# The down projection of a feed-forward block as seven products, each summed over all 22 row blocks in PSUM

## The chip, the cores and the metric

The kernel runs on one core of a Trainium2 chip. The core's engines run in parallel, each with a queue of its own in program order: TensorE (PE) multiplies matrices, VectorE (DVE) and ScalarE (ACT) work on tiles in SBUF and PSUM, GpSimd (POOL) on tiles in SBUF, and SyncE (SP) issues most of the DMA transfers. The metric is the device time of one execution in microseconds (us). All arithmetic is float32, and what a matrix multiplication reads is split into two parts of lower precision.

## The reference

A trunk of two layers on 1024 positions with 1024 features: a token mixer, a cross-attention into a memory of 256 rows, and a feed-forward block, each inside RMS norms. The change touches the feed-forward block, which each layer runs once, with `D_FF` = 2816:

```python
def rms_norm(x, g):
    return x * lax.rsqrt(jnp.mean(x * x, axis=-1, keepdims=True) + RMS_EPS) * g

def swiglu_ffn(x, w_in, w_out):
    gate, up = jnp.split(x @ w_in, 2, axis=-1)
    return (jax.nn.silu(gate) * up) @ w_out

for i in range(2):
    ...
    h = swiglu_ffn(rms_norm(x, g[4]), ffn_w_in[i], ffn_w_out[i])
    x = x + rms_norm(h, g[5])
```

Here g stands for the gains of layer i.

## The kernel before

**Up projection** (`ffn`, L440). The 2816 hidden features are 22 blocks m of 128. For each, `block(m)` makes gate and up for all 1024 positions by 84 matmuls of 128x512 (`mm7`, L438): a 2x2 block product done by seven products instead of eight, with sums and differences of the weights made on POOL (L466 to L469). The gated block, 128 features by 1024 positions, goes to DRAM in two DMAs of 256 KB each (L530), one for each half a of the positions within a tile pair.

**Down projection** (`ffn_out`, L550). It multiplies the gated H (1024 positions by 2816 features) by `w_out` (2816 by 1024). It is again a 2x2 block product by seven products: positions are split into tiles 2j and 2j+1 (a = 0, 1), features into two halves b of each group, output columns into two halves c of 512. The loop over groups is the outer one (L556): six groups of 2, 4, 4, 4, 4 and 4 row blocks. A group loads four H tiles (L564) and four W tiles (L567), and POOL makes four left combinations (L573, L575, L577, L579) and four right ones (L574, L576, L580, and L587 when product 4 is built). `unit(i)` splits the two operands of product i into a high part (a cast on ACT, L118) and a low part (a subtraction on DVE, L119). `mm` (L606) then multiplies, per j and per row block pair, three times: high by high, high by low, low by high. Within a group products follow in the order 1, 5, 6, 3, 7, 2, 4; some share a PSUM bank, and after each one of them the bank is added into the SBUF tiles `y` by DVE (L615; by an ACT copy, L612, where the output has nothing yet). The last group has j as its outer loop, and `finish` follows each output half: a sum of squares on ACT (L619) and a multiplication by the post-norm gain on POOL (L620; for the very last tile on DVE). `close` (L363) then loads the residual rows, adds (L378) and stores them. In the first layer it goes on to the next pre-norm and transposes; tiles are closed in pairs there, and one by one in the second layer.

**What sets the order.** Each engine's queue is written by a scheduler at build time from the program's order and the pools: `wr` has 3 buffers of 512 KB, `wp` 4 of each kind (wh and wl), `t4` 4, `s7` 2, A 32, PSUM 8 banks of 128x512. `later` queues small pieces of other work (the closes; `mem_in`, which normalizes and transposes the memory rows for the next layer), and `tick` lets them go on by a piece between products. `mk` starts `mem_in(1)` when the closer of the first layer's block is made, which is at the start of the last group.

Of the kernel before, what the change touches and what calls it, by code (L numbers as in the profile page):

```python
# [21 lines left out]
class Trunk:  # L22
# [332 lines left out]
    def closer(self, gpost_row, xin, xout, gpre):  # L355
# [3 lines left out]
        ready = [[], []]  # L359
# [3 lines left out]
        def close(tiles, hs, s):  # L363
# [30 lines left out]
            ready[half] += hs  # L394
# [3 lines left out]
            yield from (self.turn7 if s7_in else self.turn)(half, ready[half], gpre)  # L398
# [41 lines left out]
    def ffn(self, w_in, w_out, mk_close):  # L440
# [3 lines left out]
        hd = [self.dram([P, 2, 4, P]) for _ in range(NF)]  # L444
# [26 lines left out]
        w = lambda W, n: W[n] if isinstance(W[n], tuple) else unit(W[n])  # L471

        def block(m):
# [45 lines left out]
            nc.gpsimd.tensor_mul(h1, h1, u3)  # L519
# [8 lines left out]
            nc.vector.tensor_mul(h0, h0, a)  # L528
            for i in range(2):
                nc.sync.dma_start(hd[m][:, i], ht.rearrange('f (q a t) -> f a q t', q=4, a=2)[:, i])  # L530
# [17 lines left out]
        self.ffn_out(hd, w_out, mk_close)  # L548

    def ffn_out(self, hd, w_out, mk_close):  # L550

        nc = self.nc
        sizes = [1] + [2] * 5
        y, m0 = (None, 0)
        view = lambda t, K: t[:, :K * 512].rearrange('p (k c) -> p k c', k=K)
        for gi, K in enumerate(sizes):  # L556
            first, last = (gi == 0, gi == len(sizes) - 1)
            n = K * 512
            H, W = ({}, {})
            for b in range(2):  # L560
                for a in range(2):
                    H[a, b] = self.a32()
                    for k in range(K):
                        nc.sync.dma_start(H[a, b][:, k * 512:k * 512 + 512], hd[m0 + b * K + k][:, a].rearrange('f q t -> f (q t)'))  # L564
                    W[b, a] = self.wr.tile([P, D], F32, name='wr', tag='wr') if b else self.tmp()
                    r0 = (m0 + b * K) * P
                    nc.sync.dma_start(view(W[b, a], K), w_out[r0:r0 + K * P, a * 512:a * 512 + 512].rearrange('(k p) c -> p k c', p=P))  # L567
            H = {k: x[:, :n] for k, x in H.items()}
            W = {k: x[:, :n] for k, x in W.items()}
            E = nc.gpsimd  # L570
            s1, s2, s4 = [self.a32()[:, :n] for _ in range(3)]
            t1, t2 = [self.s7.tile([P, D], F32, name='s7', tag='s7')[:, :n] for _ in range(2)]
            E.tensor_add(s1, H[1, 0], H[1, 1])  # L573
            E.tensor_sub(t1, W[0, 1], W[0, 0])  # L574
            E.tensor_sub(s2, s1, H[0, 0])  # L575
            E.tensor_sub(t2, W[1, 1], t1)  # L576
            E.tensor_sub(s4, H[0, 1], s2)  # L577
            s3, t3, t4 = (H[1, 0], W[0, 1], W[1, 0])
            E.tensor_sub(s3, H[0, 0], s3)  # L579
            E.tensor_sub(t3, W[1, 1], t3)  # L580
            ops = {1: (H[0, 0], W[0, 0]), 5: (s1, t1), 6: (s2, t2), 3: (s4, W[1, 1]), 7: (s3, t3), 2: (H[0, 1], W[1, 0]), 4: (H[1, 1], t4)}
            units = {}

            def unit(i):
                if i not in units:
                    if i == 4:
                        E.tensor_sub(t4, t4, t2)  # L587
                    h, w = ops[i]
                    us = []
                    for j, x in enumerate((h, w)):  # L590
                        if j and (not (last and i in (7, 2, 4))):
                            hi = self.wp.tile([P, D], F32R, name='wh', tag='wh')
                            lo = self.wp.tile([P, D], F32R, name='wl', tag='wl')
                        else:
                            hi, lo = (self.a32r(), self.a32r())
                        self.split(hi[:, :n], lo[:, :n], x)
                        us.append((view(hi, K), view(lo, K)))
                    units[i] = us
                return units[i]

            def mm(ps, i, j, start):
                (hh, hl), (wh, wl) = unit(i)
                js = slice(j * P, (j + 1) * P)
                for k in range(K):
                    for q, (a, b) in enumerate(((hh[:, k, js], wh[:, k]), (hh[:, k, js], wl[:, k]), (hl[:, k, js], wh[:, k]))):
                        nc.tensor.matmul(ps, lhsT=a, rhs=b, start=start and k == 0 and (q == 0), stop=k == K - 1 and q == 2, skip_group_check=True)  # L606
            done = set()

            def add(t, c, ps):
                o = y[t][:, c * 512:c * 512 + 512]  # L610
                if first and (t, c) not in done:
                    nc.scalar.copy(o, ps)  # L612
                    done.add((t, c))
                else:
                    nc.vector.tensor_add(o, ps, o)  # L615

            def finish(t, c):
                o = y[t][:, c * 512:c * 512 + 512]
                nc.scalar.activation(self.junk, o, AF.Square, scale=1.0 / 32, accum_out=s3_[:, c:c + 1, t % nn])  # L619
                (nc.gpsimd if nn > 1 or (nn == 1 and t < 7) else nc.vector).tensor_mul(o, o, close.gpost[:, c * 512:c * 512 + 512])  # L620
# [1082 lines left out]
```

## Time and profile before

| | us |
|---|---|
| median of 3 timed executions | 3323.72 |
| lowest, highest | 3318.04, 3324.5 |
| the profiled execution | 3319.07 |
| its span, first to last instruction | 3317.1 |
| down projection, first layer | 1078.3 to 1343.0 |
| down projection, second layer | 3054.1 to 3307.7 |

The mean granted TensorE clock was 0.957. The profile gives, for each engine, the time that it was busy; a line such as L615 is a line of the kernel before. Groups of instructions name the operation with its output and inputs by tile names, the tile shape, the count, the busy time, the mean of one, and the idle time just before them with what ended it. In a list of waits "X <- Y" says that X stood idle until Y was done. "SPq" rows are DMA issues; the end of a transfer is seen in the instruction that waited for it.

### The profile page before, as it was taken

Reading aid. Unit: us, or ns where it says so; the run is one execution under the profiler, and the core shown is the slowest. Engines: PE = TensorE matmul, PEld = TensorE weight load, DVE = VectorE, ACT = ScalarE, POOL = GpSimd, SP = SyncE. Lnnn points to the kernel's source line nnn. Section 1 sums busy time; section 2 is a strip of 40 time slices with the busy share of each in tenths; the row PEclk is TensorE's granted clock in tenths of the full one; section 3 lists DMA queues with packets and bytes.
Section 4 is the critical chain, followed back from the end, with each engine's and each line's share of the span. In section 5 each row is a group of like instructions: output and inputs, shape, how many; then the busy total and the mean of one; then the engine's idle time right before and its main releaser. Section 6 shows DMA issues by size and latency. Waiting matters only on the chain. (4 is left out here: it accounts for less than half of the span.)

```text
span 3317.1 us, 44473 instructions
## 1 busy us (share of the span) xinstructions
PE 3155.1 (95%) x16586; PEld 2534.3 (76%) x16586; DVE 2023.3 (61%) x2875; ACT 1490.9 (45%) x2759; POOL 1062.2 (32%) x800
## 2 busy tenths in 40 slices
PE   8999999899999888999989999999999899999897
PEld 6888888678888666877668688787788688887666
DVE  5463545655444998755766375664545744445998
ACT  5443544533333433766753254465545533334332
POOL 0000011443334654311512242343011633334654
PEclk9999999999999999999998587899999999999999
DMA  5622544332223432744856443635544232323322
GB/s 185 203 76 70 197 146 141 113 96 83 76 77 89 140 102 76 246 126 130 286 176 171 139 106 83 168 93 175 172 159 157 65 96 83 87 79 115 108 96 95
DMA packets 446231, 421.44 MB, mean 127 GB/s; under 512 B 74560, under 2 KB 349152, under 8 KB 446016
## 3 DMA queue, kind: packets, MB, share of 16 engines
q1 hardware_dynamic: 439104, 393.44, 38.7%
q0 software_dynamic: 6912, 25.17, 2.3%
q8 instruction: 131, 2.15, 0.3%
q14 instruction: 84, 0.69, 0.1%
HBM read 313.61 MB, written 104.92 MB: 126 GB/s over the span
## 5 line engine op out<-in xcount | busy, mean ns | idle before, releaser
L438 PE MATMUL ps<-a,wh 128*128 128x512 f32 x2464 | 771.9, 398 | 6.9 <-DVE a L119 5.4
L119 DVE TENSOR_TENSOR wl<-wr,wh 128x1024 fp32r<-128x1024 f32 (+1 forms) x369 | 447.8, 1224 | 352.9 <-ACT wh L118 352.4
L118 ACT CAST wh<-wr 128x1024 fp32r<-128x1024 f32 (+1 forms) x369 | 323.4, 889 | 533.4 <-PE ps L438 179.9
L438 PEld LDWEIGHTS ps<-a,wh 128*128 128x128 f32 x2464 | 465.2, 189 | 123.8 <-DVE a L119 7.4
L438 PE MATMUL ps<-a,wl 128*128 128x512 f32 x1232 | 479.6, 397 | 0.0
L606 PE MATMUL ps<-wh,a 128*128 128x512 f32 x1136 | 381.8, 407 | 47.1 <-DVE a L615 31.6
L148 PE MATMUL ps<-a,wh 128*128 128x512 f32 (+1 forms) x848 | 333.9, 399 | 12.2 <-ACT a L118 8.6
L149 PE MATMUL ps<-a,wh 128*128 128x512 f32 (+2 forms) x848 | 328.7, 389 | 1.1 <-DVE a L119 1.1
L150 PE MATMUL ps<-a,wl 128*128 128x512 f32 (+2 forms) x848 | 327.6, 388 | 1.1 <-DVE wl L119 1.0
L148 PE MATMUL ps<-wh,a 128*128 128x512 f32 x800 | 313.8, 401 | 11.7 <-DVE a L415 7.7
L149 PE MATMUL ps<-wl,a 128*128 128x512 f32 x800 | 318.5, 398 | 0.0
L150 PE MATMUL ps<-wh,a 128*128 128x512 f32 x800 | 316.3, 399 | 0.0
L606 PEld LDWEIGHTS ps<-wh,a 128*128 128x128 f32 x1136 | 217.6, 192 | 123.3 <-DVE a L615 37.8
L438 PEld LDWEIGHTS ps<-a,wl 128*128 128x128 f32 x1232 | 233.1, 189 | 57.5 <-DVE wl L119 0.9
L119 DVE TENSOR_TENSOR wl<-s,wh 128x512 fp32r<-128x512 f32 (+1 forms) x200 | 207.6, 1050 | 76.7 <-ACT wh L118 73.8
L118 ACT CAST wh<-s 128x512 fp32r<-128x512 f32 (+1 forms) x200 | 129.7, 662 | 247.1 <-PE ps L438 86.8
L119 DVE TENSOR_TENSOR a<-a 128x1024 fp32r<-128x1024 f32 (+1 forms) x134 | 216.5, 1630 | 24.3 <-ACT a L118 20.8
L606 PE MATMUL ps<-wl,a 128*128 128x512 f32 x568 | 227.5, 401 | 0.0
L208 POOL TENSOR_TENSOR sm<-sm,mhalf 128x4 f32<-128x4 f32 (+3 forms) x60 | 67.8, 1133 | 489.1 <-DVE sm L228 423.6
L615 DVE TENSOR_TENSOR a<-ps,a 128x512 f32<-128x512 f32 x304 | 195.5, 680 | 13.8 <-PE ps L606 13.7
L148 PEld LDWEIGHTS ps<-a,wh 128*128 128x128 f32 x848 | 162.6, 193 | 50.7 <-ACT a L118 9.3
L118 ACT CAST a<-a 128x1024 fp32r<-128x1024 f32 (+1 forms) x150 | 125.3, 867 | 153.0 <-POOL a L577 53.5
(275 smaller groups left out, 5663.0 us busy)
## 6 DMA issues: line engine op xcount, KB each, us to landing
wr<-in_ffn_w_in SPq DMA_DIRECT2D x90, 512.0 KB
scr<-t SPq DMA_DIRECT2D x136, 256.0 KB
scr<-t SPq DMA_DIRECT2D x60, 512.0 KB
a<-scr SPq DMA_DIRECT2D x108, 256.0 KB
wr<-in_rw_w_rkv SPq DMA_DIRECT2D x48, 512.0 KB
t<-scr SPq DMA_DIRECT2D x36, 512.0 KB
ld<-scr SPq DMA_DIRECT2D x72, 256.0 KB
wr<-in_xa_wkv SPq DMA_DIRECT2D x32, 512.0 KB
```

The source lines that it names most:

```text
L118: self.nc.scalar.copy(hi, src)
L119: (engine or self.nc.vector).tensor_sub(lo, src, hi)
L148: nc.tensor.matmul(out, lhsT=ah, rhs=bh, start=start, stop=False)
L149: nc.tensor.matmul(out, lhsT=ah, rhs=bl, start=False, stop=False)
L150: nc.tensor.matmul(out, lhsT=al, rhs=bh, start=False, stop=stop)
L208: self.nc.gpsimd.tensor_tensor(out=r, in0=v, in1=self.mhalf[:, 0:n], op=ALU.pow)
L438: self.nc.tensor.matmul(out, lhsT=a, rhs=b, start=start and k == 0 and (i == 0), stop=k == 3 and i == 2, skip_group_check=True)
L606: nc.tensor.matmul(ps, lhsT=a, rhs=b, start=start and k == 0 and (q == 0), stop=k == K - 1 and q == 2, skip_group_check=True)
L615: nc.vector.tensor_add(o, ps, o)
```

## The change

`ffn_out` no longer loops over groups outside and products inside, but over products outside and steps inside. Each product (in the order 1, 2, 5, 6, 3, 7, 4) runs over six steps, one of one pair of row blocks and five of two, and stays in PSUM all the while; `evac` moves it out at its end. A bank that products share is read and then added to further. The W tiles stay in the A pool, and the right combinations are made in them by POOL as each product reaches them. The left combinations are made in the up projection by `out(m)`, once for each pair of row blocks, on POOL; H goes to seven DRAM tensors of 256 KB per pair, and a step loads the one that it needs through `wr`, three steps ahead. In the second layer product 4 runs tile by tile (j outermost), with its operands in the A pool. `finish` reads PSUM directly for product 4; `src is o` compares two slices made by separate calls. Closes come by even and by odd tiles in the first layer, so `ready` holds them by tile. `mem_in(1)` starts at product 7.

The diff, without `ffn_out`:

```diff
-        ready = [[], []]
+        ready = [{}, {}]
...
-            ready[half] += hs
+            ready[half].update(zip(tiles, hs))
             if len(ready[half]) < 4:
                 return
             self.fp32_in = fp32_in
-            yield from (self.turn7 if s7_in else self.turn)(half, ready[half], gpre)
+            yield from (self.turn7 if s7_in else self.turn)(half, [ready[half][t] for t in sorted(ready[half])], gpre)
             ready[half] = None
...
-    def ffn(self, w_in, w_out, mk_close):
+    def ffn(self, w_in, w_out, mk_close, late=None):
...
-        hd = [self.dram([P, 2, 4, P]) for _ in range(NF)]
+        hd = {i: self.dram([NF // 2, P, 512]) for i in range(1, 8)}
+        kept = {}
...
+        by_a = lambda x: x.rearrange('f (q a t) -> f a q t', a=2, t=P)
+
+        def gated(m, half):
+
+            if m not in kept:
+                kept[m] = self.a32()
+            return kept[m].rearrange('f (a q t) -> f a q t', a=2, t=P)[:, :, 2 * half:2 * half + 2]
+
+        def out(m):
+
+            c, x = m // 2, kept[m]
+            if m % 2 == 0:
+                nc.sync.dma_start(hd[1][c], x[:, :512])
+                return
+            e = kept.pop(m - 1)
+            del kept[m]
+            h00, h10, h01, h11 = (e[:, :512], e[:, 512:], x[:, :512], x[:, 512:])
+            nc.sync.dma_start(hd[2][c], h01)
+            nc.sync.dma_start(hd[4][c], h11)
+            cb = self.a32()
+            s1, s4 = (cb[:, :512], cb[:, 512:])
+            nc.gpsimd.tensor_add(s1, h10, h11)
+            nc.sync.dma_start(hd[5][c], s1)
+            nc.gpsimd.tensor_sub(h10, h00, h10)
+            nc.sync.dma_start(hd[7][c], h10)
+            nc.gpsimd.tensor_sub(h00, s1, h00)
+            nc.sync.dma_start(hd[6][c], h00)
+            nc.gpsimd.tensor_sub(s4, h01, h00)
+            nc.sync.dma_start(hd[3][c], s4)
...
-            nc.gpsimd.tensor_mul(h1, h1, u3)
+            nc.gpsimd.tensor_mul(gated(m, 1), by_a(h1), by_a(u3))
...
-            nc.vector.tensor_mul(h0, h0, a)
-            for i in range(2):
-                nc.sync.dma_start(hd[m][:, i], ht.rearrange('f (q a t) -> f a q t', q=4, a=2)[:, i])
+            nc.vector.tensor_mul(gated(m, 0), by_a(h0), by_a(a))
+            out(m)
...
-            if n == 2:
-                mem_in(1)
...
-        T.ffn(I['ffn_w_in'][i], I['ffn_w_out'][i], mk(3 * i + 2))
+        T.ffn(I['ffn_w_in'][i], I['ffn_w_out'][i], mk(3 * i + 2), None if i else lambda: mem_in(1))
```

And `ffn_out` as it is now, with the line numbers of the changed kernel:

```python
L579 def ffn_out(self, hd, w_out, mk_close, late):
L581     nc = self.nc
L582     steps = [(0, 1)] + [(c, 2) for c in range(1, D_FF // P // 2, 2)]
L583     NS = len(steps)
L584     seq = [(i, n) for i in (1, 2, 5, 6, 3, 7, 4) for n in range(NS)]
L585     view = lambda t, K: t[:, :K * 512].rearrange('p (k c) -> p k c', k=K)
L586     wv = w_out.rearrange('(c b p) n -> b p c n', b=2, p=P)
L587     W, H, U = ({}, {}, {})
L588     y = [self.a32() for _ in range(NT)]
L589     close = mk_close()
L590     nn = 2 if close.follow else 1
L592     def load(q):
L593         i, n = seq[q]
L594         c, K = steps[n]
L595         H[q] = self.wr.tile([P, D], F32, name='wr', tag='wr')
L596         nc.sync.dma_start(view(H[q], K), hd[i][c:c + K].rearrange('k f n -> f k n'))
L597         if i in (1, 2, 5, 6):
L598             b, a = {1: (0, 0), 2: (1, 0), 5: (0, 1), 6: (1, 1)}[i]
L599             W[b, a, n] = self.a32()
L600             nc.sync.dma_start(view(W[b, a, n], K), wv[b][:, c:c + K, a * 512:a * 512 + 512])
L602     def unit(q, resident=False):
L603         i, n = seq[q]
L604         K = steps[n][1]
L605         N = K * 512
L606         w = lambda b, a: W[b, a, n][:, :N]
L607         E = nc.gpsimd
L608         if i == 5:
L609             E.tensor_sub(w(0, 0), w(0, 1), w(0, 0))
L610         elif i == 6:
L611             E.tensor_sub(w(0, 0), w(1, 1), w(0, 0))
L612         elif i == 7:
L613             E.tensor_sub(w(0, 1), w(1, 1), w(0, 1))
L614         elif i == 4:
L615             E.tensor_sub(w(1, 0), w(1, 0), w(0, 0))
L616         src = {1: (0, 0), 5: (0, 0), 6: (0, 0), 2: (1, 0), 4: (1, 0), 3: (1, 1), 7: (0, 1)}[i]
L617         us = []
L618         for x in (H.pop(q)[:, :N], w(*src)):
L619             if resident:
L620                 hi, lo = (self.a32r(), self.a32r())
L621             else:
L622                 hi = self.wp.tile([P, D], F32R, name='wh', tag='wh')
L623                 lo = self.wp.tile([P, D], F32R, name='wl', tag='wl')
L624             self.split(hi[:, :N], lo[:, :N], x)
L625             us += [view(hi, K), view(lo, K)]
L626         U[q] = us
L628     def mm(ps, q, j):
L629         i, n = seq[q]
L630         hh, hl, wh, wl = U[q]
L631         js = slice(j * P, (j + 1) * P)
L632         for k in range(steps[n][1]):
L633             for z, (a, b) in enumerate(((hh[:, k, js], wh[:, k]), (hh[:, k, js], wl[:, k]), (hl[:, k, js], wh[:, k]))):
L634                 nc.tensor.matmul(ps, lhsT=a, rhs=b, start=i in (1, 2, 5) and n == 0 and k == 0 and z == 0, stop=n == NS - 1 and k == steps[n][1] - 1 and z == 2, skip_group_check=True)
L635     sums, done = ({}, {})
L637     def finish(t, c, src):
L639         group = (t % 2, t // 2 // nn)
L640         tiles = [2 * (group[1] * nn + g) + group[0] for g in range(nn)]
L641         if group not in sums:
L642             sums[group] = self.sums(nn)
L643             done[group] = 0
L644         s, s3 = sums[group]
L645         o = y[t][:, c * 512:c * 512 + 512]
L646         nc.scalar.activation(self.junk, src, AF.Square, scale=1.0 / 32, accum_out=s3[:, c:c + 1, tiles.index(t)])
L647         (nc.gpsimd if src is o else nc.vector).tensor_mul(o, src, close.gpost[:, c * 512:c * 512 + 512])
L648         done[group] += 1
L649         if done[group] == 2 * nn:
L650             self.later(close(tiles, [y[x] for x in tiles], s))
L652     def evac(i, j, A, B):
L653         o = lambda r, c: y[2 * j + r][:, c * 512:c * 512 + 512]
L654         if i == 1:
L655             nc.scalar.copy(o(0, 0), A)
L656         elif i == 2:
L657             nc.vector.tensor_add(o(0, 0), B, o(0, 0))
L658             finish(2 * j, 0, o(0, 0))
L659         elif i == 5:
L660             nc.scalar.copy(o(1, 1), B)
L661         elif i == 6:
L662             nc.scalar.copy(o(0, 1), A)
L663         elif i == 3:
L664             nc.vector.tensor_add(o(0, 1), B, o(0, 1))
L665             finish(2 * j, 1, o(0, 1))
L666         elif i == 7:
L667             nc.vector.tensor_add(o(1, 1), A, o(1, 1))
L668             finish(2 * j + 1, 1, o(1, 1))
L669         else:
L670             finish(2 * j + 1, 0, A)
L671     AHEAD = 3
L672     for q in range(AHEAD):
L673         load(q)
L674     unit(0)
L675     A, B = ([None] * 4, [None] * 4)
L676     by_tile = not close.follow
L677     for q, (i, n) in enumerate(seq):
L678         if q + AHEAD < len(seq):
L679             load(q + AHEAD)
L680         if q + 1 < len(seq):
L681             unit(q + 1, by_tile and seq[q + 1][0] == 4 and seq[q + 1][1] < NS - 2)
L682         if late and i == 7 and n == 0:
L683             late()
L684         if by_tile and i == 4:
L685             continue
L686         X = A if i in (1, 6, 7, 4) else B
L687         for j in range(4):
L688             if i in (1, 2, 5) and n == 0:
L689                 X[j] = self.bank()
L690             mm(X[j], q, j)
L691             if n == NS - 1:
L692                 evac(i, j, A[j], B[j])
L693             self.tick()
L694         del U[q]
L695     if by_tile:
L696         for j in range(4):
L697             for q in range(6 * NS, 7 * NS):
L698                 mm(A[j], q, j)
L699                 if q % 2:
L700                     self.tick()
L701             evac(4, j, A[j], None)
L702             self.tick(4)
```

Three lists show where the instructions go. The first is SyncE's queue around the end of the first layer's up projection, before: wr and t4 tiles are W loads, scr tiles H blocks in DRAM, the last one (scr32) of block 21.

```order
L567 DMA wr_8081<-in_ffn_w_out 128x512 [waits DMAHW5_49,DVE_49,Pool_49]
L567 DMA wr_8297<-in_ffn_w_out 128x2x512 [waits DMAHW0_49,DVE_49]
L567 DMA t4_8069<-in_ffn_w_out 128x512 [waits DMAHW7_49,DMAHW6_49,Pool_49]
L530 DMA scr31_5000<-t4_7830 128x4x128 [waits DVE_49]
L530 DMA scr31_5000<-t4_7830 128x4x128
L567 DMA t4_8073<-in_ffn_w_out 128x512 [waits DMAHW7_49,DMAHW1_49,DMAHW0_49]
L567 DMA t4_8287<-in_ffn_w_out 128x2x512 [waits DMAHW2_49,DMAHW6_49,DVE_49,Pool_49]
L567 DMA t4_8292<-in_ffn_w_out 128x2x512 [waits DMAHW3_49,Pool_49]
L567 DMA wr_8302<-in_ffn_w_out 128x2x512 [waits DMAHW4_49,DVE_49]
L530 DMA scr32_5001<-t4_7961 128x4x128 [waits DMAHW5_49,DVE_49]
```

The same place now: scr12 to scr17 are H operands of the products, a_8174 the W of the first step, a_8178 that of the second.

```order
L490 DMA scr12_4981<-a_8115 128x512 [waits DMAHW5_49,DVE_49]
L491 DMA scr14_4983<-a_8115 128x512 [waits DMAHW6_49]
L600 DMA a_8174<-in_ffn_w_out 128x512 [waits DMAHW7_49,PE_49]
L495 DMA scr15_4984<-a_8153 128x512 [waits DMAHW0_49,Pool_49]
L600 DMA a_8178<-in_ffn_w_out 128x2x512 [waits DMAHW1_49,DMASW2_49,PE_49]
L600 DMA a_8182<-in_ffn_w_out 128x2x512 [waits DMAHW2_49,PE_49]
L497 DMA scr17_4986<-a_7984 128x512 [waits DMAHW3_49,Pool_49]
L600 DMA a_8194<-in_ffn_w_out 128x2x512 [waits DMAHW4_49,PE_49]
```

W loads that stood ahead of the last block's store now stand behind the stores of the last pair, which wait for DVE and then for POOL.

The second is VectorE's queue in the first layer's down projection, before, in mid-projection: L119 are the splits, L615 the additions of PSUM banks (ps) into y (the a tiles).

```order
L615 TENSOR_TENSOR a_8101<-ps_8388,a_8101 128x512 [waits DVE_49,PE_49]
L119 TENSOR_TENSOR wl_8550<-wr_8297,wh_8549 128x1024 [waits Activation_49]
L615 TENSOR_TENSOR a_8096<-ps_8316,a_8096 128x512 [waits PE_49]
L119 TENSOR_TENSOR wl_8619<-t4_8584,wh_8618 128x1024 [waits Activation_49]
L615 TENSOR_TENSOR a_8098<-ps_8332,a_8098 128x512 [waits PE_49]
L119 TENSOR_TENSOR a_8615<-a_8581,a_8614 128x1024 [waits DMAHW5_49,DMAHW4_49,Activation_49]
L615 TENSOR_TENSOR a_8100<-ps_8340,a_8100 128x512 [waits PE_49]
```

The same queue now, at the end of product 2 and the start of product 5: L657 are additions of product 2 and L647 the multiplications by the gain (gb).

```order
L119 TENSOR_TENSOR wl_8582<-wr_8504,wh_8581 128x512 [waits DMAHW1_49,DVE_49,Activation_49]
L119 TENSOR_TENSOR wl_8586<-a_8174,wh_8585 128x512 [waits Activation_49]
L657 TENSOR_TENSOR a_8162<-ps_8416,a_8162 128x512 [waits PE_49]
L657 TENSOR_TENSOR a_8164<-ps_8420,a_8164 128x512 [waits PE_49]
L647 TENSOR_TENSOR a_8162<-a_8162,gb_8170 128x512 [waits Activation_49]
L657 TENSOR_TENSOR a_8166<-ps_8424,a_8166 128x512 [waits PE_49]
L647 TENSOR_TENSOR a_8164<-a_8164,gb_8170 128x512 [waits Activation_49]
L657 TENSOR_TENSOR a_8168<-ps_8428,a_8168 128x512 [waits PE_49]
L119 TENSOR_TENSOR wl_8633<-wr_8540,wh_8632 128x1024 [waits DMAHW2_49,Activation_49]
L647 TENSOR_TENSOR a_8166<-a_8166,gb_8170 128x512 [waits Activation_49]
L119 TENSOR_TENSOR wl_8637<-a_8178,wh_8636 128x1024 [waits Activation_49]
L647 TENSOR_TENSOR a_8168<-a_8168,gb_8170 128x512 [waits Activation_49]
```

The additions that alternated with splits throughout are gone from mid-product and stand in fours at a product's end, with the multiplications, which were POOL's.

More of the change, by code (lines that the diff above doesn't have):

```diff
@@ new lines, in ffn_out, with load @@
+        wv = w_out.rearrange('(c b p) n -> b p c n', b=2, p=P)
+        W, H, U = ({}, {}, {})
+        y = [self.a32() for _ in range(NT)]
+        close = mk_close()
+        nn = 2 if close.follow else 1
+        def load(q):
+            i, n = seq[q]
+            c, K = steps[n]
+            H[q] = self.wr.tile([P, D], F32, name='wr', tag='wr')
+            nc.sync.dma_start(view(H[q], K), hd[i][c:c + K].rearrange('k f n -> f k n'))
+            if i in (1, 2, 5, 6):
+                b, a = {1: (0, 0), 2: (1, 0), 5: (0, 1), 6: (1, 1)}[i]
+                W[b, a, n] = self.a32()
+                nc.sync.dma_start(view(W[b, a, n], K), wv[b][:, c:c + K, a * 512:a * 512 + 512])
@@ new lines, in mm @@
+        def mm(ps, q, j):
+            i, n = seq[q]
+            hh, hl, wh, wl = U[q]
+            js = slice(j * P, (j + 1) * P)
+            for k in range(steps[n][1]):
+                for z, (a, b) in enumerate(((hh[:, k, js], wh[:, k]), (hh[:, k, js], wl[:, k]), (hl[:, k, js], wh[:, k]))):
+                    nc.tensor.matmul(ps, lhsT=a, rhs=b, start=i in (1, 2, 5) and n == 0 and k == 0 and z == 0, stop=n == NS - 1 and k == steps[n][1] - 1 and z == 2, skip_group_check=True)
+        sums, done = ({}, {})
@@ new lines, in finish @@
+        def finish(t, c, src):
+            group = (t % 2, t // 2 // nn)
+            tiles = [2 * (group[1] * nn + g) + group[0] for g in range(nn)]
+            if group not in sums:
+                sums[group] = self.sums(nn)
+                done[group] = 0
+            s, s3 = sums[group]
+            o = y[t][:, c * 512:c * 512 + 512]
+            nc.scalar.activation(self.junk, src, AF.Square, scale=1.0 / 32, accum_out=s3[:, c:c + 1, tiles.index(t)])
+            (nc.gpsimd if src is o else nc.vector).tensor_mul(o, src, close.gpost[:, c * 512:c * 512 + 512])
+            done[group] += 1
+            if done[group] == 2 * nn:
+                self.later(close(tiles, [y[x] for x in tiles], s))
@@ new lines, in ffn_out @@
+        AHEAD = 3
+        for q in range(AHEAD):
+            load(q)
+        unit(0)
+        A, B = ([None] * 4, [None] * 4)
+        by_tile = not close.follow
+        for q, (i, n) in enumerate(seq):
+            if q + AHEAD < len(seq):
+                load(q + AHEAD)
+            if q + 1 < len(seq):
+                unit(q + 1, by_tile and seq[q + 1][0] == 4 and seq[q + 1][1] < NS - 2)
+            if late and i == 7 and n == 0:
+                late()
+            if by_tile and i == 4:
+                continue
+            X = A if i in (1, 6, 7, 4) else B
+            for j in range(4):
+                if i in (1, 2, 5) and n == 0:
+                    X[j] = self.bank()
+                mm(X[j], q, j)
+                if n == NS - 1:
+                    evac(i, j, A[j], B[j])
+                self.tick()
+            del U[q]
@@ L683, in params @@
+        if by_tile:
+            for j in range(4):
+                for q in range(6 * NS, 7 * NS):
+                    mm(A[j], q, j)
+                    if q % 2:
+                        self.tick()
+                evac(4, j, A[j], None)
+                self.tick(4)
     def params(self, parts):
```

169 lines of the change are left out of this document (47 added, 122 removed).

## The prediction

> **What bounds the kernel now.** First the page, for the whole span.
>
> ```profile
> span 3317.1 us, 44473 instructions
> PE 3155.1 (95%) x16586; PEld 2534.3 (76%) x16586; DVE 2023.3 (61%) x2875; ACT 1490.9 (45%) x2759; POOL 1062.2 (32%) x800
> ```
>
> TensorE is busy for 95% of the span, so there is a ceiling on any gain; but this is a mean over stages. The busy time by stretch gives them apart: 100 us of an up projection, then the two down projections (columns: length; PE, PEld, DVE, ACT, POOL busy; clock; DMA share; GB/s).
>
> ```profile
> 800.00:900.00 100.00, 100.00 (x428) 80.41 (x427) 48.49 (x57) 35.09 (x62) 35.78 (x26) 1.00 0.29 81
> 1078.30:1343.00 264.70, 232.14 (x953) 178.47 (x951) 251.50 (x251) 106.12 (x149) 144.73 (x59) 0.96 0.35 113
> 3054.10:3307.70 253.60, 225.08 (x912) 171.34 (x911) 242.02 (x243) 90.87 (x120) 144.69 (x61) 0.98 0.32 105
> ```
>
> In the up projection PE is never idle: 100.00/428 = 0.2336 us a matmul, DVE 48%. In the down projections DVE is busy 95% (251.50/264.70 and 242.02/253.60) and PE is not full. The second, part of whose first group ran earlier, holds 912 matmuls: at 0.2336 they need 213.0 us, so 40.6 are lost. The first holds 41 small ones more, about half a matmul each (41 × 0.12 = 4.9): 264.7 − 213.0 − 4.9 = 46.8 lost. **Ceiling: 87.4 us**. The groups of instructions and the waits (second down projection; for waits: total, times, longest) say what DVE does and who waits.
>
> ```profile
> L615 DVE TENSOR_TENSOR a<-ps,a 128x512 f32<-128x512 f32 x152 | 97.8, 681 | 7.8 <-PE ps L606 7.8
> L119 DVE TENSOR_TENSOR a<-a 128x1024 fp32r<-128x1024 f32 x35 | 71.7, 2052 | 1.7 <-POOL a L579 1.7
> PE ps L606 <- DVE a L615: 19.6, 19, 4.1
> PE ps L606 <- DVE a L119: 4.6, 2, 3.9
> PE ps L606 <- ACT a L118: 4.1, 2, 2.6
> ```
>
> The L615 additions take 97.8 of DVE's 242 us and are the largest thing PE waits for. The rest of the loss is the slow clock behind such stops (0.96, 0.98) and PE's own issue gaps.
>
> **The change, part by part**, against the profiled execution (3319.07 us, of which 3317.1 are span; the median shown, 3323.72, is 4.65 above it).
>
> *Removed:* 152 additions per down projection become 12 (at the ends of products 2, 3 and 7), since a product stays in PSUM over all 22 row blocks. 140 × 0.681 = 95.3 us of DVE leave each. Of the POOL work, four left combinations per group move to the up projection.
>
> *What a step then needs.* One step is one product over two pairs: 24 matmuls, 24 × 0.2336 = 5.6 us.
>
> ```profile
> 3070.93 1.21 DVE L119 TENSOR_TENSOR wl<-t,wh 128x1024 fp32r<-128x1024 f32 x1
> 3071.51 1.05 ACT L118 CAST wh<-s 128x1024 fp32r<-128x1024 f32 x1 [2.49 <-PE ps L606]
> ```
>
> Each step needs two casts and two splits. The buffers (four wh, four wl) hold two steps, so the chain starts when the step before last is finished: cast 1.05 and two splits 2 × 1.21 = 3.5 us. The low part is wanted only at the fifth matmul, so the limit is 5.6 + 4 × 0.2336 = 6.5: slack 3.0. With the splits at the mean seen in this stage (2.05, beside POOL) the chain is 5.2, still inside. So mid-product PE should run full, and the ceiling is what I start from. Four terms come off it.
>
> *(1) The transition from up to down.* Before, W for the first group was issued ahead of the last block's stores, and product 1 of it ran between that block's products. Now W stands behind those stores in SP's queue.
>
> ```profile
> 3053.69 0.39 PE L438 MATMUL ps<-a,wl 128*128 128x512 f32 x1
> 3053.79 0.37 SPq L567 DMA_DIRECT2D wr<-in_ffn_w_out  x1
> 3053.93 0.62 ACT L118 CAST wh<-t 128x512 fp32r<-128x512 f32 x1 [0.98 <-issue]
> 3054.12 0.69 DVE L528 TENSOR_TENSOR t<-t,ps 128x512 f32<-128x512 f32 x1 [0.36 <-PE ps L438]
> 3054.84 0.92 SPq L530 DMA_DIRECT2D scr<-t  x2
> 3058.13 2.40 POOL L580 TENSOR_TENSOR t<-wr,t 128x1024 f32<-128x1024 f32 x1 [1.55 <-DMA wr<-in_ffn_w_out]
> ```
>
> The last up matmul ends at 3054.08; the multiplication that feeds the stores ends 0.73 us later, two store issues take 0.92. A 512 KB load took 3053.79 to 3058.13 = 4.34 until its reader began. The one needed first is 256 KB; one such was read 2.64 after its issue:
>
> ```profile
> 3040.56 4.32 SPq L567 DMA_DIRECT2D t<-in_ffn_w_out  x2
> 3043.20 1.28 POOL L574 TENSOR_TENSOR s<-t,t 128x512 f32<-128x512 f32 x1 [6.05 <-DMA t<-in_ffn_w_out]
> ```
>
> Of 2.64 to 4.34 I take 3.5, then the cast of 0.62: 0.73 + 0.92 + 3.5 + 0.62 = 5.8 us. Nothing covers it: PE has no other work there. Queued behind that store on SP are all W loads and the second half of the last pair's H, so all of it shifts together. A stop of this size also costs clock:
>
> ```profile
> 1314.00 1.97 PE L843 MATMUL ps<-ident,a 128*128 128x128 f32 x8 [7.75 <-DVE a L833]
> 1315.62 0.78 PE L606 MATMUL ps<-wh,a 128*128 128x512 f32 x1
> 1318.71 0.62 PE L606 MATMUL ps<-wh,a 128*128 128x512 f32 x2
> ```
>
> After 7.75 us of idleness eight transposes took 1.97 for about 1.0 (8 × 0.12), and eight matmuls filled 1315.62 to 1318.71, 3.09 for 1.87: 2.2 us dearer. (1) is 8.0 each, **16 together**; bounds 0 (hidden by an earlier issue) and 10 each (4.34, and the second step's load late by as much again as its 256 KB more take).
>
> [...]
>
> *(2) The product ends.* The additions and gain multiplications now come four at a time among the splits.
>
> ```profile
> L620 DVE TENSOR_TENSOR a<-a,gb 128x512 f32<-128x512 f32 x2 | 2.1, 1074 | 0.3 <-ACT junk L619 0.3
> L378 DVE SCALAR_TENSOR_TENSOR t<-a,sm,t 128x1024 f32<-128x1024 f32 (+1 forms) x9 | 13.0, 1450 | 0.6 <-POOL sm L208 0.4
> L612 ACT COPY a<-ps 128x512 f32<-128x512 f32 x16 | 8.8, 593 | 4.2 <-PE ps L606 3.9
> 1311.66 2.28 DVE L833 SCALAR_TENSOR_TENSOR a<-a,sm 128x1024 f32<-128x1024 f32 x1
> ```
>
> All 16 multiplications go to DVE: the test for POOL compares two slices made afresh, which are never the same object. At an end: 4 × 0.68 + 4 × 1.07 + the next step's splits 2.4 = 9.4 against 5.6; 3.8 over, less the slack 3.0: 0.8. Behind product 3 two closes (L378, 1.45 each) stand among the splits: 3.7. So 0.8 + 3.7 + 0.8, and ACT's copies hold a cast up about 0.25 at three ends: 6.1 each, and in the first 2 × 1.3 for the memory rows, whose scaling (L833 now) moves from the last group to product 7, taken at L378's pace and not at its crowded 2.28; their three loads move on SP to stand between H loads, where nothing of PE's waits for them. **15 together.** Bounds: 0, if the slack takes all; and without slack 3.8 + 6.7 + 3.8 and the copies each, with the rows 33 together.
>
> *(3) POOL beside DVE.*
>
> ```profile
> 3058.36 2.72 DVE L119 TENSOR_TENSOR a<-a 128x512 fp32r<-128x512 f32 x1 [1.22 <-ACT a L118]
> L587 POOL TENSOR_TENSOR wr<-wr,s 128x1024 f32<-128x1024 f32 (+1 forms) x6 | 14.7, 2446 | 26.8 <-DVE wl L119 21.5 <-issue 5.3
> ```
>
> A half split took 2.72 beside POOL's L580 (above): 2.40 of it is POOL's duration, as if it had waited that out. POOL keeps 24 right combinations per down projection, 24 × 2.45 = 59 us. One per step is inside the slack of 3.0; two are not. I take **3 us each, 6**: near the bound 0, for the row of the mean split (2.05) says that one meeting is usual; the other bound is rival B.
>
> *(4) Supply.* Every H is now a DMA of its own: 7 × 11 × 256 KB and 11.5 MB of W, 31.7 MB in some 216 us = 147 GB/s.
>
> ```profile
> 1350.00:1400.00 50.00, 50.00 (x308) 44.77 (x308) 39.56 (x50) 41.66 (x69) 9.96 (x17) 0.98 0.78 252
> ```
>
> 252 GB/s were moved elsewhere with PE full. I take **3 each, 6** for a late load where steps are short; bounds 0 and rival C.
>
> *In the up projection* the stores and POOL's four more combinations per pair lie beside a full PE with POOL at 36%: 44 × 1.3 = 57 us in some 430 raise it to about 50%. Nothing. *At the end* the last addition goes:
>
> ```profile
> 3307.95 0.69 DVE L615 TENSOR_TENSOR a<-ps,a 128x512 f32<-128x512 f32 x1 [0.62 <-PE ps L606]
> ```
>
> **Sum:** 87.4 − 16 − 15 − 6 − 6 + 0.7 = 45 us. 3319.07 − 45 = 3274; as executions shown run from here to 5 above, **3275**.
>
> **The rivals.**
> *A, ends hidden:* the slack takes (2) to (4) and only the transition remains: 87.4 − 16 + 0.7 = 72, **3247**. For it: DVE falls to 242.0 − 95.3 + 15.0 (14 more multiplications) = 162 us of 216. Against: its additions now come in bursts. 0.10.
> *B, the splits are the new bound:* two steps of buffers are too few when both splits meet POOL. The slowest split seen is
>
> ```profile
> L119 DVE TENSOR_TENSOR a<-t,a 128x1024 fp32r<-128x1024 f32 x1 | 3.0, 3040 | 0.0
> ```
>
> two of these and the cast make 7.1 against 6.5: 0.6 a step. Over 70 wide steps 36 to 42 us more, less what (3) holds: about **3310**. Against: a combination comes in only 46 of them. 0.10. [...]
> *C, slower, W starves H:* W loads wait for no compute and stand in SP's order ahead of H, so 14.9 MB (W 8.9, H 3.9, the last stores 1.6, closing rows 0.5) are issued before the H of product 2's last step, due about 57 us after the start. Without loss that is 262 GB/s. Each down projection loses its gain of about 23 us when they take 80, below 186 GB/s, and at the 105 to 113 of the present stage 14.9 MB take 135 us: 78 − 23 = 55 worse each, **about 3430**. Against: the 252 above, at a DMA share of only 0.78. 0.06.
> *D, the wait only moves:* PE waits for splits as it did for additions, **3319**. Against: DVE loses a third of its work. 0.04.
>
> **How the numbers follow.** Forecast 0.70 (3255 to 3295), A 0.10, B 0.10, C 0.06, D 0.04. The range reaches A and B, 3247 to 3310, leaving out C and D. A difference of 0.2% (7 us) is about what a measurement can tell. Faster by more: forecast, A and most of B, 0.89; within: D and a little of B, 0.05; slower: 0.06.
>
> **What would show it.** Right: PE full in mid-product; a stop of 5 to 7 us ahead of L634's first matmul; stops of 1 to 4 us at the ends of products 2, 3 and 7; no more than a few us of PE waiting for a load; DVE near 75% there. Wrong: many short waits of L634 for L119 (B), waits of the L118 casts for H loads of tens of us (C), or any PE idle time in the up projection.

## The result and the profile after

| | before | changed |
|---|---|---|
| median of 17 executions each | 3323.72 us | 3289.33 us |
| lowest, highest | 3306.62, 3346.7 | 3277.86, 3313.54 |
| ratio, 95% interval | | 0.9913, 0.989 to 0.9935 |
| profiled execution, span | 3317.1 | 3275.9 |

The time lies in the range, and the change is faster by 29 us by the ratio (22 to 37). That is some six tenths of the 45 forecast, though the two profiled executions differ by 41.2: the changed kernel's (3277.86) is the fastest of its 17, so the pair of profiles flatters the change. The page of the changed kernel:

```profile
span 3275.9 us, 44234 instructions
PE 3132.8 (96%) x16586; PEld 2532.3 (77%) x16586; DVE 1855.3 (57%) x2625; ACT 1487.1 (45%) x2751; POOL 1028.6 (31%) x810
```

Busy time by stretch, the two down projections, from the last matmul of the up projection to the last of the down (columns as in the prediction):

```profile
1076.30:1317.10 240.80, 220.80 (x943) 177.79 (x943) 161.96 (x131) 108.38 (x158) 79.24 (x34) 0.97 0.48 164
3028.70:3268.80 240.10, 220.05 (x924) 175.57 (x924) 156.60 (x125) 93.71 (x125) 84.54 (x35) 0.97 0.47 160
```

DVE fell from 251.5 and 242.0 us to 162.0 and 156.6: it bounds neither projection as a whole any more. They last 240.8 and 240.2 us instead of 264.7 and 253.8, while at 924 × 0.2336 their matmuls need 215.8. What is left can be read from the stops of PE. Timeline of PE in the first down projection, every matmul that it stood before (start, duration, then the idle time and what ended it):

```profile
1082.25 2.08 PE L634 MATMUL ps<-wh 128*128 128x512 f32 x4 [5.94 <-ACT wh L118]
1135.18 0.50 PE L634 MATMUL ps<-wl,wh 128*128 128x512 f32 x1 [0.42 <-DVE wl L119]
1147.04 0.47 PE L634 MATMUL ps<-wh 128*128 128x512 f32 x1 [1.47 <-DVE a L657]
1149.04 0.50 PE L634 MATMUL ps<-wh 128*128 128x512 f32 x1 [0.36 <-DVE a L657]
1150.73 0.50 PE L634 MATMUL ps<-wh 128*128 128x512 f32 x1 [0.73 <-DVE a L657]
1153.60 0.50 PE L634 MATMUL ps<-wl,wh 128*128 128x512 f32 x1 [0.98 <-DVE wl L119]
1160.88 0.50 PE L634 MATMUL ps<-wl,wh 128*128 128x512 f32 x1 [1.54 <-DVE wl L119]
1189.62 0.80 PE L634 MATMUL ps<-wl,wh 128*128 128x512 f32 x1 [3.94 <-DVE wl L119]
1202.96 0.50 PE L634 MATMUL ps<-wl,wh 128*128 128x512 f32 x1 [0.83 <-DVE wl L119]
1209.64 0.50 PE L634 MATMUL ps<-wl,wh 128*128 128x512 f32 x1 [0.93 <-DVE wl L119]
1256.43 0.51 PE L634 MATMUL ps<-wl,wh 128*128 128x512 f32 x1 [2.63 <-DVE wl L119]
1290.51 0.49 PE L634 MATMUL ps<-wl,wh 128*128 128x512 f32 x1 [0.23 <-DVE wl L119]
```

The first is the transition, 5.94 us. The three with L657 are a wait that nobody forecast: product 5 needs the PSUM banks of product 2, which DVE has not added out yet. The rows from 1153 to 1210 lie in products 5 and 6, where the low part is late in many steps; the row at 1256 is the start of product 7, behind the closes. What DVE and POOL did in product 6 (the timeline of all engines but PE, those two picked out):

```profile
1201.79 3.38 POOL L613 TENSOR_TENSOR a<-a 128x1024 f32<-128x1024 f32 x1
...
1202.83 3.41 DVE L119 TENSOR_TENSOR wl<-wr,wh 128x1024 fp32r<-128x1024 f32 x1
1205.12 6.72 POOL L615 TENSOR_TENSOR a<-a 128x1024 f32<-128x1024 f32 x2
1206.16 3.42 DVE L119 TENSOR_TENSOR wl<-a,wh 128x1024 fp32r<-128x1024 f32 x1
...
1209.51 3.41 DVE L119 TENSOR_TENSOR wl<-wr,wh 128x1024 fp32r<-128x1024 f32 x1
```

A split that takes 1.22 alone (the mean of 37 in the run without combinations, below) takes 3.4 here, and so does each combination. The operations of the two engines start in turn, POOL's at 1201.79 and 1205.12, DVE's at 1202.83, 1206.16 and 1209.51, and each takes nearly as long as both together (1.22, and 2.41 for a combination that went first, at 1182.80). Two splits are then 6.8 us a step, against 5.6 of matmuls.

The stages of the profiles, in us ("up + down" from the first up matmul to the last down one; "between" from the end of the first layer's down projection to the second layer's up projection, which holds the second layer's mixer and cross-attention; "tail" is what follows the last down matmul):

| | up + down 1 | between | up + down 2 | tail |
|---|---|---|---|---|
| before | 721.7 | 1253.7 | 711.1 | 9.2 |
| before, second profile | 718.8 | 1241.8 | 712.7 | 9.1 |
| changed | 695.7 | 1256.3 | 695.4 | 7.1 |
| changed, second profile | 695.1 | 1261.0 | 695.6 | 7.1 |

(The up projection is 2 us shorter now in each layer, since 12 matmuls of product 1 ran inside it before.) The feed-forward stages gain 26.0, 15.7 and 2.1 = 43.8 us. They repeat within 1 us in the changed kernel and within 3 us in the kernel before. What varies most lies between them, in work that the change hardly touches. It does move some: 22 small matmuls of 128x256 (L148 to L150), 2.6 us at 0.117 each, ran inside the first down projection before and now run behind it, so that much of the 26.0 is not a gain.

### The profile page after: what moved, and what is told of

Its sections match the earlier page's. It is cut to its first block, busy times and chain, and to the rows that moved or that the text cites. A ratio compares the mean times of both kernels' runs of the same rounds, so it can differ in the third digit from the quotient of the medians.

```text
span 3275.9 us, 44234 instructions
## 1 busy us (share of the span) xinstructions
PE 3132.8 (96%) x16586; PEld 2532.3 (77%) x16586; DVE 1855.3 (57%) x2625; ACT 1487.1 (45%) x2751; POOL 1028.6 (31%) x810
## 4 chain that ended last, share of the span: by engine, by line
PE 80%; DVE 8%; DMA 4%; ACT 3%; issue 3%; POOL 1%; SPq 0%; DVEq 0%; POOLq 0%; ACTq 0%
PE ps L438 24%; PE ps L148 11%; PE ps L150 11%; PE ps L149 11%; PE ps L634 9%; PE ck L1428 4%; DVE wl L119 4%; PE ps L1319 2%; PE ck L1441 2%; PE ps L1343 1%; DMA wr<-scr 1%; DVE a L119 1%; ACT wh L118 1%; DMA ld<-scr 1%; PE ps L262 1%
## 5 line engine op out<-in xcount | busy, mean ns | idle before, releaser
L119 DVE TENSOR_TENSOR wl<-wr,wh 128x1024 fp32r<-128x1024 f32 (+1 forms) x417 | 513.9, 1242 | 479.8 <-ACT wh L118 478.9
L148 PE MATMUL ps<-a,wh 128*128 128x512 f32 (+1 forms) x848 | 331.5, 396 | 13.9 <-ACT a L118 7.4
L150 PE MATMUL ps<-a,wl 128*128 128x512 f32 (+2 forms) x848 | 326.2, 386 | 1.6 <-DVE wl L119 1.5
L148 PE MATMUL ps<-wh,a 128*128 128x512 f32 x800 | 316.3, 402 | 9.3 <-DVE a L1523 4.8
L149 PE MATMUL ps<-wl,a 128*128 128x512 f32 x800 | 317.8, 397 | 0.0
L150 PE MATMUL ps<-wh,a 128*128 128x512 f32 x800 | 316.3, 398 | 0.0
L634 PE MATMUL ps<-wl,wh 128*128 128x512 f32 x588 | 236.1, 402 | 22.0 <-DVE wl L119 22.0
L119 DVE TENSOR_TENSOR wl<-s,wh 128x512 fp32r<-128x512 f32 x176 | 199.7, 1148 | 70.6 <-ACT wh L118 67.0
L634 PE MATMUL ps<-wh,wl 128*128 128x512 f32 x588 | 233.4, 397 | 0.0
L634 PE MATMUL ps<-wh 128*128 128x512 f32 x588 | 196.8, 397 | 17.7 <-ACT wh L118 12.5
L148 PEld LDWEIGHTS ps<-a,wh 128*128 128x128 f32 x848 | 161.5, 192 | 51.5 <-ACT a L118 8.5
L118 ACT CAST wh<-s 128x512 fp32r<-128x512 f32 x176 | 106.3, 619 | 201.7 <-PE ps L438 70.9
L150 PEld LDWEIGHTS ps<-a,wl 128*128 128x128 f32 (+1 forms) x848 | 162.0, 191 | 37.1 <-DVE wl L119 2.8
L149 PEld LDWEIGHTS ps<-a,wh 128*128 128x128 f32 (+1 forms) x848 | 162.8, 192 | 31.7 <-DVE a L119 1.6
L148 PEld LDWEIGHTS ps<-wh,a 128*128 128x128 f32 x800 | 151.2, 189 | 46.2 <-DVE a L1523 5.2
```

The costliest lines, as they stand in the source:

```text
L118: self.nc.scalar.copy(hi, src)
L119: (engine or self.nc.vector).tensor_sub(lo, src, hi)
L148: nc.tensor.matmul(out, lhsT=ah, rhs=bh, start=start, stop=False)
L149: nc.tensor.matmul(out, lhsT=ah, rhs=bl, start=False, stop=False)
L150: nc.tensor.matmul(out, lhsT=al, rhs=bh, start=False, stop=stop)
L634: nc.tensor.matmul(ps, lhsT=a, rhs=b, start=i in (1, 2, 5) and n == 0 and k == 0 and z == 0, stop=n == NS - 1 and k == steps[n][1] - 1 and ...
```

## The experiments

Each is the changed kernel with one edit, unless said otherwise; ratios are to the kernel before, with 95% intervals, and stages are from the profile of the run.

**The changed kernel once more** (`after_again`).

> The changed kernel once more, for a second profile and more times. Theory 1 (the shortfall of the median against the one profile lies outside the down projections): its two down projections last 240.6 and 240.1 us again within 2 us, PE idle in them 20 us each, and what differs in the span lies in the second layer's token mixer, which the change does not touch. Theory 2 (the down projection itself varies, with loads that come late): a down projection is longer by 5 us or more in this profile, with PE waiting behind ACT or DVE that wait for a load.

Ratio 0.9915 (0.9884 to 0.9946), median 3298.55 of 11. Down projections 239.9 and 240.5, PE's stops 21.2 and 20.1; between them 1261.0 instead of 1256.3. The projections differ by less than 1 us between the two profiles, so theory 1 holds as far as they go.

**An early load** (`w_early`):

```diff
             if not first:
                 self.mm7(a, w(W, 1), X[1], True)
+            if m == NF - 1:
+                del X[1]
+                for n in range(3):
+                    pre[n] = self.a32()
+                    c, K = (0, 1) if n == 0 else (2 * n - 1, 2)
+                    nc.sync.dma_start(pre[n][:, :K * 512].rearrange('p (k c) -> p k c', k=K), wv[0][:, c:c + K, :512])
...
+                if i == 1 and n in pre:
+                    W[b, a, n] = pre.pop(n)
+                    return
```

> The right operands of the first three steps are loaded in the last up block, into tiles that the first up product frees, so ahead of the last stores on SP. Theory 1 (the transition is a wait for that load): PE's stop ahead of the first down matmul, 5.94 and 6.54 us, falls under 1 us and the slow clock behind it is gone, 7 to 8 us a layer, 14 to 16 in all. Theory 2 (the burst of loads bounds the start): the stop moves to the second or third step and less than 5 us is won in all.

Ratio 0.9804 (0.9762 to 0.9846). PE's timeline at the seam (L644 is the down matmul there):

```profile
1073.45 0.39 PE L644 MATMUL ps<-wh,wl 128*128 128x512 f32 x1
1073.68 0.63 PE L438 MATMUL ps<-a,wh 128*128 128x512 f32 x2
...
1076.25 0.40 PE L438 MATMUL ps<-a,wl 128*128 128x512 f32 x1
1076.48 1.08 PE L644 MATMUL ps<-wh 128*128 128x512 f32 x4
```

The first step runs ahead of the last up product, and the second follows without a stop. Up + down fell from 695.7 to 686.9 and from 695.4 to 688.0: 8.8 + 7.4 = 16.2 us, as theory 1 had it. The profiles bear that out: the spans differ by 20.9 us, 3.0 of them in the stretch between, which comes out in yet another order and took 1253.3 us. The ratio moved by more, 1.1% or 36 us. The executions of this kernel had a higher granted clock, 0.959 in the median against 0.954 for those of the changed kernel in the same series; that the edit raised it is not shown.

**No combinations** (`no_comb`): the four `E.tensor_sub` of `unit` (L609 to L615) become `pass`.

> The 24 right combinations per down projection on POOL are left out (the products take uncombined weights), so POOL has nothing beside the splits. Theory 1 (POOL and DVE hold each other up by whole operations): no split of 128x1024 above 1.3 us in a down projection, the gaps in products 5 and 6 (1.0, 1.5, 3.9, 0.8, 0.9 in the first layer, 1.0, 1.5, 1.9, 0.5, 0.9, 0.9 in the second) go, 15 to 20 us in all, part of the wait for the banks at product 5 with them. Theory 2 (these gaps come from late loads): they stay, and the time falls by less than 5 us.

Ratio 0.9798 (0.9752 to 0.9845); down projections 226.5 and 226.5, so 14.3 + 13.7 = 28.0 us. DVE's wide splits in the first one, by form, changed kernel first, then this one:

```profile
L119 DVE TENSOR_TENSOR wl<-wr,wh 128x1024 fp32r<-128x1024 f32 x37 | 62.0, 1677 | 53.6 <-ACT wh L118 53.4
```

```profile
L119 DVE TENSOR_TENSOR wl<-wr,wh 128x1024 fp32r<-128x1024 f32 x37 | 45.2, 1223 | 73.4 <-ACT wh L118 73.1
```

In the first projection the gaps of products 5 and 6 went but for one of 0.24 us, and those for the banks too; 2.64 at product 7 and 0.24 at product 4 stayed. Behind the transition PE waited for no load. Theory 1 holds, and the effect was dearer than it said.

**Combinations on DVE** (`dve_comb`):

```diff
-            E = nc.gpsimd
+            E = nc.vector
```

> The changed kernel with its 24 right combinations per down projection on DVE instead of POOL. Theory 1 (the loss of 14 us a projection that went when the combinations were left out is POOL and DVE holding each other up): DVE has 24 x 1.2 = 29 us more a projection, but a step's chain is 1.2 + 1.05 + 2.4 = 4.7 us against 6.5, so it hides; no wide split above 1.3 us, the down projections fall from 240.8 and 240.2 to about 228 each, 22 to 26 us in all. Theory 2 (it is the combination's own time that delays the split, wherever it runs): they stay above 235.

Ratio 0.9801 (0.9765 to 0.9838); down projections 228.8 and 230.1: 22.1 us. DVE's splits and one of the four lines of combinations in the first projection:

```profile
L119 DVE TENSOR_TENSOR wl<-wr,wh 128x1024 fp32r<-128x1024 f32 x37 | 45.2, 1223 | 54.2 <-ACT wh L118 54.0
...
L613 DVE TENSOR_TENSOR a<-a 128x1024 f32<-128x1024 f32 x5 | 6.1, 1219 | 0.0
```

The combinations cost 1.22 each on DVE, where they took 3.05 to 3.34 on POOL, and no split is long. So most of the loss, 22.1 of the 28.0 us, came from the two engines working at the same time, and not from the work itself.

**A copy by ACT at the end of product 2** (`late_add`):

```diff
-                nc.vector.tensor_add(o(0, 0), B, o(0, 0))
+                if j % 2 == 0:
+                    self.hold = self.s7.tile([P, D], F32, name='s7', tag='s7')
+                hb = self.hold[:, j % 2 * 512:j % 2 * 512 + 512]
+                nc.scalar.copy(hb, B)
+                nc.vector.tensor_add(o(0, 0), hb, o(0, 0))
```

> At the end of product 2 an ACT copy takes the bank to SBUF, and DVE adds from there. Theory 1 (PE waits at product 5 because the banks are freed by additions that stand behind splits in DVE's queue): the three waits of 1.47, 0.36 and 0.73 us go, up to 2.5 us a layer, of which the copies in ACT's queue (4 x 0.6, ahead of a cast) may give half back: 0 to 5 us in all. Theory 2 (the splits are late there anyway): PE waits as long for the low parts and the time is the same.

Down projections 240.9 and 243.7, none shorter. The ratio, 0.986 (0.9806 to 0.9915), is better by 0.5% than the changed kernel's, but the two intervals overlap, and no stage that the edit touches bears it out. PE's stops in the first projection:

```profile
1146.20 0.50 PE L634 MATMUL ps<-wh 128*128 128x512 f32 x1 [0.38 <-ACT s L660]
1148.90 0.79 PE L634 MATMUL ps<-wh 128*128 128x512 f32 x1 [1.73 <-ACT s L660]
```

The wait for the bank moved to the copies, which stand in ACT's queue behind squares that wait for DVE (3.01 us for the first, until 1144.95). Theory 1 fell: with DVE late, freeing the banks from ACT did not help here.

**Gain multiplications on POOL** (`pool_mul`):

```diff
-            (nc.gpsimd if src is o else nc.vector).tensor_mul(...)
+            (nc.gpsimd if c or t % 2 == 0 else nc.vector).tensor_mul(...)
```

> The changed kernel with 12 of the 16 gain multiplications of a projection on POOL, as the source means them, instead of DVE. Theory 1 (POOL's work costs by holding splits up, DVE has time): the down projections are no shorter, 240 to 245 us. Theory 2 (the multiplications in DVE's queue delay the splits at the ends of products 2, 3 and 7, as the prediction had it with 0.8, 3.7 and 0.8): 3 to 5 us shorter each.

In the one execution that there is, the down projections last 245.3 and 242.7 us, longer by 4.5 and 2.5 (the stop at product 7 is 4.81 instead of 2.63). As far as one execution tells, the comparison that sends them to DVE helps the kernel.

**Both edits** (`best`), the early load and the combinations on DVE.

> The early load of the first three right operands and the combinations on DVE together. Theory 1 (two separate terms, 16 us and 22 to 26 us): up and down projection together fall from 695.7 and 695.4 us to about 675 each, the time to about 0.975 of the kernel before. Theory 2 (one hides behind the other): less than 30 us below the changed kernel in these two stages together.

Ratio 0.9752 (0.9714 to 0.979), median 3232.41. Up + down 674.7 and 676.4: 21.0 + 19.0 = 40.0 us below the changed kernel, against 16.2 + 22.1 = 38.3 for each alone. The terms add up. The down projections last 217.7 and 219.5, 2 and 4 us above their matmuls.

**The change in one layer alone** (`only_ffn2`, `only_ffn1`): the other layer calls the kernel before's `ffn` and `ffn_out`.

> The change in the second layer alone, the first layer's feed-forward block as before, so that the second layer's mixer is scheduled behind what it was before. Theory 1 (in the changed kernel the mixer between the two blocks, scheduled in another order and free to vary from run to run, takes 10 to 17 us more in the median): here the mixer keeps its 1254 to 1260 us; the gain is that of the second block's stages, 2.0 + 13.6 + 2.1 = 17.7 us, ratio 0.9947, in the median as in the profile. Theory 2 (the mixer only varies by itself, the same in both): the same here, and in the run with the first layer alone a ratio of 0.992.

> The change in the first layer alone, the second layer's feed-forward block as before. By the stages it gains 2.2 + 23.9 = 26 us up to the end of the first down projection. Theory 1 (the mixer behind it gives back 10 to 17 us in the median): ratio 0.995 to 0.997. Theory 2 (no systematic loss there): ratio 0.992.

Second layer alone: 0.9942 (0.9913 to 0.997), between 1258.9. First layer alone: 0.9974 (0.9944 to 1.0004), between 1282.0. The first layer's 26 us shrink to 9 in the ratio (-1 to 19 by its interval), and the two gains add up to the whole one's (0.58% + 0.26% = 0.84%; measured 0.87%). Theory 1 fits both; the first layer alone decides, where theory 2's 0.992 lies outside the interval.

**The kernel before once more** (`before_again`).

> The kernel before, once more, as any other: it tells what a ratio of 1 looks like here, and gives a second profile of the stages. Theory 1 (the mixer in the changed kernel's order takes longer than in this one): the mixer with what lies around it again 1254 to 1260 us, against 1256 to 1282 in the four profiles in the changed kernel's order. Theory 2 (both vary alike): over 1262 here. Ratio 1.000 within 0.003 by both.

Ratio 0.9999 (0.9963 to 1.0035). Between: 1241.8, below what either theory had. In the kernel before's order the stretch has now 1253.7, 1258.9 and 1241.8; in the changed kernel's (the same matmuls in the same order as far as the second down projection: both its profiles, `no_comb`, `only_ffn1`) 1256.3, 1261.0, 1267.6 and 1282.0. The means differ by 15, the single ones by up to 26 within one order.

**Both edits and the last product by tile pair in the first layer** (`best_bt`): `by_tile = True`.

> The early load and the combinations on DVE, and in the first layer too the last product runs tile pair by tile pair, so that the closes of odd tiles come apart. Theory 1 (the 6.3 us stop behind the first down projection is the last group's closes, which all come in the last 5.6 us now): the stop falls to 4 us or less, 2 to 4 us with its slow clock. Theory 2 (the stop is the length of the last close itself, as before the change): it stays at 6 us, and the time is that of the kernel with the two edits, 0.975 of the one before.

Ratio 0.9785 (0.9749 to 0.982), no better than the kernel with the two edits (0.9752; the intervals overlap). The stop behind the first down projection in the kernel before, the changed one and this one:

```profile
1346.90 0.45 PE L262 MATMUL ps<-ident,a 128*128 128x128 f32 x1 [3.78 <-DVE a L391]
```

```profile
1329.10 0.66 PE L262 MATMUL ps<-ident,a 128*128 128x128 f32 x2 [6.29 <-DVE a L391]
```

```profile
1316.91 0.66 PE L262 MATMUL ps<-ident,a 128*128 128x128 f32 x2 [12.98 <-ACT a L389]
```

It doubled (the kernel with the two edits has 6.29 as well); both theories are wrong. What PE waits for is now the last close's scaling on ACT, and ACT has the mixer's first work ahead of it.

## Why the prediction came out as it did

**What bounds it, and the ceiling: right.** DVE's 95% and the additions were the bound. With the two edits 217.7 and 219.5 us are left of 264.7 and 253.8, so nearly all of the 87.4 us was there to be had. The sum left out that all 924 matmuls of a projection run behind the up projection now, 12 × 0.2336 = 2.8 us more in each; the up projections, 2 us shorter, pay for most of it.

**(1) Transition: right**, mechanism and size: 5.94 and 6.54 against 5.8 idle, 16.2 us against 16 by the early load. The slow clock was sized well too: the ten matmuls from 1082.25 on took 4.42 us, at a granted clock of 0.50, where ten take 2.34, 2.1 dearer against the 2.2 in the sum; from 1086.67 the clock was 1.00 again.

**(3) POOL beside DVE: the term that was mis-sized.** Forecast 6, measured 28.0 by leaving the combinations out. The step that failed is "One per step is inside the slack of 3.0; two are not. I take 3 us each": it put the combinations one to a step, as the source builds them. POOL's queue doesn't keep to steps: it holds those of products 6, 7 and 4 one behind the other, and POOL makes them as soon as W is there. The order of the changed kernel on POOL in the first layer had told so:

```
L611 TENSOR_TENSOR a_8178<-a_8769,a_8178 128x1024 [waits DVE_49]
L615 TENSOR_TENSOR a_8330<-a_8330,a_8178 128x1024 [waits Pool_49]
L611 TENSOR_TENSOR a_8182<-a_8806,a_8182 128x1024 [waits DVE_49]
L615 TENSOR_TENSOR a_8366<-a_8366,a_8182 128x1024 [waits Pool_49]
L611 TENSOR_TENSOR a_8194<-a_8847,a_8194 128x1024 [waits DMAHW3_49,DVE_49]
L613 TENSOR_TENSOR a_8629<-a_8847,a_8629 128x1024 [waits DMASW6_49,PE_49]
```

Product 4's L615 and product 7's L613 stand among product 6's L611. Rival B's mechanism ("both splits meet POOL") is what happened, in two products of seven. The sign "PE full in mid-product" failed there, and the sign named for B, waits of L634 for L119, showed.

**(2) Product ends: too dear, and partly another wait.** Forecast 15. At product 5 PE waited 2.56 us for banks, which the sum did not have, and it did so because of (3): without combinations that is gone, and what stays in the first projection is 2.64 at product 7 and twice 0.24. The closes among the splits were the right place (3.7 forecast), the seams without closes cost almost nothing; a multiplication took 0.72 on DVE, not the 1.07 taken.

**(4) Supply: nothing.** Forecast 6. No stop of PE but the transition's goes back to a load, and without combinations 226.5 is 215.8 + 8 + 2.7, which leaves nothing for it. Rival C's burst of W did no harm: 293 GB/s were moved in the first 57 us of the first projection, more than the 262 that C asked for.

So (2) to (4) were 27 in the sum and about 33 in fact (28.0 and twice 2.7), by errors that went against each other: the forecast of 45 met the 43.8 of the stages partly by luck.

**What no term had: the work behind the first layer.** "PE full" was followed to the end of each projection. Behind the first one the stop for the closes is 6.29 us instead of 3.78. Both odd groups end in the last step now; that this is the reason was argued, and the run that took them apart made the stop longer. And the second layer's mixer comes out in another order, though nothing in it was edited: the scheduler places it behind what came before. That the median gains less than the profiles can be placed here: with the feed-forward stages fixed at the profile's values, 3289.33 leaves some 11 us more than the profiled execution for what lies around them, this stretch above all by how much it varies between the profiles. Shown is that the first layer alone gives 9 us in the ratio and not 26, and that the projections hardly vary.

An estimate takes the clock out: each execution's time multiplied by its mean granted clock. The 17 of the changed kernel, 3277.86 to 3313.54 us, become 3140 to 3153, so most of their spread goes with the clock. The medians become 3171 for the kernel before and 3157 with the first layer alone, in one series: a gain of 14 us, still not 26. So a chance of the clock does not explain the missing 12; the 2.6 us of moved matmuls and the 2.6 us that the stop is longer in that run are part of it. That the mixer's order makes the rest, and the 15 us between the means of the seven profiles, was only argued: no run held the order of the mixer fixed against the change.

## What to carry to other kernels

Before costing vector work that GpSimd runs beside, read GpSimd's own queue and not the source: here the combinations of three products ran in a lump, and in the lump both engines took turns, a split of 1.22 us and a combination of 2.41 taking 3.4 each. Where such work is small, try it on the vector engine too: here a combination took 1.22 us there, instead of 3.3 on GpSimd and a split drawn out from 1.2 to 3.4. And when a profile pair shows more than the median, see where the profiled execution stands among the others, and split the span by stages: a repeat of the stages that the change touches tells whether the effect is there, and one edit in each place alone tells where it is given back.

## What the runs showed of the hardware

**What one meeting cost went with which engine started first.** The same split and the same combination meet in product 6 in both profiles of the changed kernel:

```profile
1182.80 2.41 POOL L611 TENSOR_TENSOR a<-a 128x1024 f32<-128x1024 f32 x1 [15.22 <-DMA a<-in_ffn_w_out]
1182.92 3.37 DVE L119 TENSOR_TENSOR wl<-wr,wh 128x1024 fp32r<-128x1024 f32 x1 [4.58 <-ACT wh L118]
```

```profile
1182.87 1.23 DVE L119 TENSOR_TENSOR wl<-wr,wh 128x1024 fp32r<-128x1024 f32 x1 [4.58 <-ACT wh L118]
1182.90 3.46 POOL L611 TENSOR_TENSOR a<-a 128x1024 f32<-128x1024 f32 x1 [15.39 <-DMA a<-in_ffn_w_out]
```

With POOL 0.12 us ahead the split took 3.37 us and the combination 2.41; with DVE 0.03 us ahead the split took 1.23 and the combination 3.46. PE's next stop was 3.94 us in the first and 1.86 in the second.

**The mixer's variation went with the granted clock.** Two executions with the same matmuls in the same order (the changed kernel, then the first layer alone). The stretches begin and end at the same matmuls in both; the third number from the end is the granted clock:

```profile
1800.03:1880.18 80.15, 78.62 (x595) 55.63 (x594) 39.40 (x112) 26.72 (x50) 23.48 (x45) 0.72 0.54 157
2060.08:2130.12 70.04, 65.01 (x708) 54.58 (x707) 46.87 (x133) 33.22 (x80) 24.65 (x32) 0.91 0.53 148
```

```profile
1797.78:1887.50 89.72, 89.07 (x596) 62.63 (x594) 39.60 (x112) 27.04 (x50) 23.65 (x45) 0.62 0.50 142
2069.31:2158.84 89.53, 84.66 (x707) 71.43 (x706) 47.21 (x133) 33.39 (x80) 24.11 (x33) 0.67 0.41 116
```

The second stretch takes 89.53 us at 0.67 instead of 70.04 at 0.91, with PE idle for 5 us in both. Over the mixer (from 1640.07 to 2260.11 in the first) the second execution is 24 us longer, and PE's idle time in it is no longer (22 against 25 us). Nor does it take another chip: the eleven executions of the changed kernel once more, all on one chip, run from 3281.82 us at a clock of 0.960 to 3318.32 at 0.947. Why the clock differs from one execution to the next stays open. The differences are larger than most of the edits here are worth.
